# A decoder block on one core: split projection weights stored by one token block and loaded as halves by the next two, feed-forward sums held back, raw keys in another pool

## The chip, the cores and the metric

The kernel runs on one NeuronCore of a Trainium2 chip. The metric is the device time of one execution in microseconds. Every run is compared with the kernel before on the same chip.

The core's engines are called as in the profile: PE (TensorE, matmuls; PEld is its loading of weights), DVE (VectorE), ACT (ScalarE), POOL (GpSimd) and SP (SyncE, which here only issues DMAs). "PEq", "SPq" and so on are an engine's own sequencer.

## The reference, cut to what matters

One layer: two token mixers side by side (attention in a sliding window, and an mLSTM), merged by gates, then a feed-forward part. S = 2048 tokens, D = 1024. Shift, scale and gate of both halves come from a vector c.

```python
mod = c @ w_ada[l] + b_ada[l]
shift_m, scale_m, gate_m, shift_f, scale_f, gate_f = jnp.split(mod, 6, axis=-1)
h = modulate(rms_norm(x, g_pre_mix[l]), shift_m, scale_m)
proj = h @ w_in[l]
q_a, k_a, v_a, q_m, k_m, v_m, o_m, i_m, f_m, g_a, g_m = jnp.split(proj, split_points, axis=-1)
q_a = rope(q_a.reshape(B, S, N_Q_HEADS, HEAD_DIM), positions)
k_a = rope(k_a.reshape(B, S, N_KV_HEADS, HEAD_DIM), positions)
y_a = sliding_window_attention(q_a, k_a, v_a, attn_sinks[l])
...
merged = sigmoid(g_a) * (y_a @ w_branch_attn[l]) + sigmoid(g_m) * (y_m @ w_branch_mlstm[l])
mix = merged @ w_out[l]
x = x + gate_m[:, None, :] * rms_norm(mix, g_post_mix[l])
h2 = modulate(rms_norm(x, g_pre_ffn[l]), shift_f, scale_f)
ff = (silu(h2 @ w_ffn_gate[l]) * (h2 @ w_ffn_up[l])) @ w_ffn_down[l]
x = x + gate_f[:, None, :] * rms_norm(ff, g_post_ffn[l])
```

## The kernel before

**Products.** A float32 product is made of three matmuls of rounded numbers (`mm3`): each operand is a rounded half `hi` and a remainder `lo`, and hi*hi + hi*lo + lo*hi are summed. For weights the halves are made on the chip by `split`: ACT casts the raw tile to whi (L264 where the heads of q are put in pairs, L267 otherwise), and DVE subtracts it to get wlo (L265, L268). The matmuls of projections read "acc<-whi,big" and "acc<-wlo,big" in the trace.

**Blocks and stages.** The tokens are four blocks of 512 (b = 0 to 3; the words of the change call them one to four), in two superblocks of two. Each superblock runs, for each of its blocks, the projections of q (512 columns), of keys, values and the mLSTM's pre-gates (kv, 264 columns) and of the mLSTM's values (vm, 512 columns). Block 0 has its own start; in blocks 1 and 3 kv comes ahead of q, in block 2 q ahead of kv. Then come the remaining projections of both blocks in pairs, the mLSTM, the branch outputs and w_out. In the trace, the projections of block 1 lie at about 100 to 166 us, those of blocks 2 and 3 at about 693 to 870. The feed-forward part is the second half of the span.

**A token group.** `token_group` makes one such projection in four parts of two 128-row slices of the weight. A part is 24 matmuls (4 tokens' tiles x 2 slices x 3 products); four accumulators stay open for the group, and in the last part each is evacuated by ACT: q at L778 into a tx buffer, kv at L805, vm at L829 into a tx buffer and from there to memory at L830.

**What sets the order.** `run2` goes through a list of parts: the raw tile is loaded by SP (L298; kv at L784 and L785; the later pairs at L1864), then split, then its matmuls, with the loads and splits of the next parts issued ahead. There are two raw buffers (1.08 MB), and four split buffers of 512 KB, which is two pairs of halves. Beside the parts run streams, generators that `spawn` starts and a model of elapsed time steps: rotation and transposes of q and keys, the attention, the mLSTM, and `ada_stream`. A stream's work thus lands between the matmuls of the parts. Instructions of one engine run in the order of the program. SP issues all its DMAs in order and one that waits holds those behind it.

**Pools.** tx has nine buffers of 512 columns, used by q's evacuation and rotation, vm, residual rows and `ada_stream`'s weights; the raw keys and values of blocks 1 to 3 are in tx too (L804), those of block 0 in ld, a pool of four that the mLSTM's loads use later. A key tile is held until its rotation, its transpose and its stores to the attention's memory tile `at_d` (L798, L816, L818) are through. The attention of a block loads keys, values and q from there as `at` (L910), makes scores (mix<-at), masks (L943), takes the softmax on ACT (L958), transposes (L217, from tm) and multiplies with the values (mix<-tm,at).

**`ada_stream`** makes the feed-forward's scale, shift and gate from w_ada: a 256 KB load into tx each (L442), and a step later one DVE sum (L433). It is started in block 0's output and has a step each 9000 ns of the model's time; block 3 finishes it.

Of the kernel before, what the change touches and what calls it, by code (L numbers as in the profile page):

```python
# [19 lines left out]
P = 128  # L20
# [53 lines left out]
def decoder_block(ctx: ExitStack, tc: tile.TileContext, a: dict, out: bass.AP, dbg=None):  # L74
# [49 lines left out]
    def tx(shape, dtype=F32):  # L124
        return tpool.tile(shape, dtype, tag="tx", name=nm("tx"), bufs=9)
# [154 lines left out]
    def piece(raw, view, shape, mms, pair_heads=False):  # L280
        return Part(raw, lambda: split(view(raw.tile), shape, pair_heads), mms)
# [33 lines left out]
            for j in range(2):  # L315
                yield feature_tile(raw, lambda t, j=j: t[:, :, j * P:(j + 1) * P], k, i0 + j, rhs, evac)

    def token_group(srcs, nk, n, lhs, evac, pair_heads=False, stagger=1):

        acc = []  # L320
        srcs = list(srcs)
        held = []

        def make(si, k0, kc):
            def mms(wt):
                if not acc:
                    acc.extend(acc_tile() for _ in range(NT))
                held.append((wt, k0, kc))
                if len(srcs) - stagger <= si < len(srcs) - 1:
                    return  # L330
                for t in range(NT):
                    for w_, k0_, kc_ in held:
                        for j in range(kc_):
                            kk = k0_ + j
                            mm3(acc[t][:, :n], lhs(kk, t), (w_[0][:, j, :], w_[1][:, j, :]), kk == 0, kk == nk - 1)
                            yield
                    if si == len(srcs) - 1:
                        evac(t, acc[t])
                held.clear()
            return mms  # L340

        for si, (raw, view, k0, kc) in enumerate(srcs):
            yield piece(raw, view, [kc, n], make(si, k0, kc), pair_heads)

    def srcs_rows(w, nk, c0):
        for k0 in range(0, nk, 4):
# [80 lines left out]
    def ada_terms(acc, raw, k0, kn):  # L427
        for k in range(kn):
# [3 lines left out]
            else:  # L432
                V.scalar_tensor_tensor(acc, raw[:, k, :], c_, acc, op0=ALU.mult, op1=ALU.add)  # L433

    def ada_stream(parts, gap):
        for part, kind in parts:
            for ch in range(2):
                c0 = part * D + ch * 512
                acc = tm([P, 512])
                for k in range(KD):  # L440
                    raw = tx([P, 1, 512])
                    nc.sync.dma_start(raw, w_ada[:, c0:c0 + 512].rearrange("(p k) c -> p k c", k=KD)[:, k:k + 1, :])  # L442
                    yield gap
                    ada_terms(acc, raw, k, 1)
                if kind == "gate":
                    br = tx([1, 512])
                    nc.sync.dma_start(br, a["b_ada"][:, c0:c0 + 512])
                    yield gap
                    V.tensor_tensor(acc[0:1, :], acc[0:1, :], br, op=ALU.add)
                ada_tail(acc, part, ch, kind)  # L450
                yield gap
# [249 lines left out]
    def ld(shape, dtype=F32):  # L701
        t = kvp.tile([P, 512], dtype, tag="ld", name=nm("ld"), bufs=4)
        return t.rearrange("p (k c) -> p k c", k=shape[0])
# [24 lines left out]
    om_d = [tc.dram_tile([P, MH, TB], F32, name=f"om_d{i}") for i in range(NBLK)]  # L728
    g_d = [tc.dram_tile([P, 2, KD, TB], F32, name=f"g_d{i}") for i in range(NBLK)]
    y_d = [tc.dram_tile([P, 4, 4, TB], F32, name=f"y_d{i}") for i in range(NBLK)]  # L730
    LOGC = math.log(MD ** -0.5)
    LOG2 = math.log(2.0)

    def superblock(sb):
# [3 lines left out]
        def lhs_h(b):  # L738
            def lhs(kk, t):
                return tuple(p_[:, kk % 4, t * P:(t + 1) * P] for p_ in HC[f"{kk // 4 + 1}{b % 2 + 1}"])  # L740
            return lhs
# [58 lines left out]
        def evac_kv(b):  # L800
            before = [v_last]

            def evac(t, ps):
                raw = ld([1, 512])[:, 0, :] if b == 0 else tx([P, 392])  # L804
                A.copy(raw[:, :264], ps[:, :264])  # L805
                v, dv = raw[:, 128:256], raw[:, 264:392]
                n = b * NT + t
                y = rope(raw, HKV, b, t)
                for i in range(2):
                    A.copy(gt[:, t, 32 * i:32 * i + 4], raw[:, 256 + 4 * i:260 + 4 * i])  # L810
                V.tensor_tensor(dv, v, before[0], op=ALU.subtract)
                before[0] = v
                if t == NT - 1:
                    A.copy(v_last, v)
                    before[0] = v_last
                nc.sync.dma_start(at_d[n][:, AT_V + P:], dv)  # L816
                if n + 1 < S // P:
                    nc.sync.dma_start(at_d[n + 1][:, AT_V:AT_V + P], v)  # L818
                R["qk"].append(spawn(k_stream(n, y)))
            return evac  # L820

        def q_kv(b):
            raw_kv = Raw(load_kv)
            return token_group(srcs_rows(w_in, KD, C_Q), KD, 512, lhs_h(b), evac_q(b), pair_heads=True), token_group([(raw_kv, (lambda r, j=j: r[:, j:j + 2, :]), j, 2) for j in range(0, KD, 2)], KD, 264, lhs_h(b), evac_kv(b))

        def vm(b):
            def evac(t, ps):
                v = tx([P, 512])
                A.copy(v, ps)  # L829
                nc.sync.dma_start(vm_d[b][:, t, :], v)  # L830
            yield from token_group(srcs_rows(w_in, KD, C_VM), KD, 512, lhs_h(b), evac)


        def gates(b):
# [403 lines left out]
        def outputs(b):  # L1238

            def evac_a(i, ps):  # L1240
                g_ = R["g", b, 0, i // 4][:, i % 4, :]
                V.scalar_tensor_tensor(g_, g_, 1.0, ps, op0=ALU.add, op1=ALU.mult)

            m = {}

            def m_part(i, h):
                if (i, h) not in m:
                    m[i, h] = big([4, TB], F32R)
                return m[i, h]

            def evac_m(i, ps):
                g_ = R["g", b, 1, i // 4][:, i % 4, :]
                hi, lo = (m_part(j, i // 4)[:, i % 4, :] for j in range(2))
                V.scalar_tensor_tensor(g_, g_, 1.0, ps, op0=ALU.add, op1=ALU.mult)
                V.tensor_tensor(g_, g_, R["g", b, 0, i // 4][:, i % 4, :], op=ALU.add)
                A.copy(hi, g_)
                V.tensor_tensor(lo, g_, hi.bitcast(F32), op=ALU.subtract)

            def before_a():
                load_g(b, 1)  # L1260
                gate_tanh(b, 0)

            def before_m():
                end_chunks(NT * (b % 2 + 1))
                load_y(b, 2)
                if b + 1 == NBLK:
                    finish(R_ada)
                    open_hc()
                    R["hc"] = spawn(h_combine(0, *HC_FROM_MIXER), L_HC)
            yield before_a  # L1270
            first, second, *more = branch_tiles(w_ba, True, lambda: (R["y", b, 0], R["y", b, 1]), evac_a)
            yield first
            yield second
            yield more[0]
            yield before_m
            yield from more[1:]
            yield lambda: gate_tanh(b, 1)
            yield from branch_tiles(w_bm, False, lambda: (R["y", b, 2], R["y", b, 3]), evac_m)

            def before_out():  # L1280
                if b == 0:
                    finish(R["ada_m"])
                    R_ada.append(spawn(ada_stream([(4, "scale"), (3, "shift"), (5, "gate")], 9000.0)))
                if b == b1 and b + 1 < NBLK:
                    HC.clear()
                    hps[b + 1] = spawn(hprep(b + 1))
                    rope_tables(sb + 1)
                R["gg"] = big([2, D])[:, 0, :]
                nc.sync.dma_start(R["gg"], gg_m_d)
                if b == b0:  # L1290
                    end_attention(2 * NT)
                    load_y(b1, 0)
                    load_g(b1, 0)

            yield before_out

            def gg(c):
                return R["gg"][:, c]

            yield from residual_out(KD, lambda kk, t: tuple(m[i, kk // 4][:, kk % 4, t * P:(t + 1) * P] for i in range(2)),  # L1300
                                    a["w_out"][0], big, load_rows(x_d[b * TB:(b + 1) * TB, :], b + 1 == NBLK), gg, x1[b],
                                    None if b + 1 == NBLK else x1n[b])
# [25 lines left out]
            first.update(kv=kv0, evac=q_raw, rope=q_rope, rest=q_rest)  # L1328
        else:
            yield start  # L1330
            yield from q0
            yield from kv0
            yield lambda: attend(b0)
# [13 lines left out]
        def start_f():  # L1347
# [2 lines left out]
            hps["t"] = spawn(hsums(("T1", "T3")))  # L1350

        yield start_f
        pairs = [("om", 0), ("qk", 0), ("om", 1), ("qk", 1), ("ga", 0), ("qk", 2), ("ga", 1), ("qk", 3),
                 ("ga", 2), ("ga", 3), ("gm", 0), ("gm", 1), ("gm", 2), ("gm", 3)]
        for i, (kind, p) in enumerate(pairs):
# [855 lines left out]
```

## Time and profile before

| | us |
|---|---|
| median of three runs | 2673.64 (2673.51 to 2677.0) |
| the profiled execution | 2673.95 |
| its span | 2672.2 |
| PE busy | 2620.8 |
| DVE busy | 1964.5 |
| ACT busy | 1304.4 |
| POOL busy | 136.3 |

The profiled execution has 1.75 us outside its span. Its mean granted PE clock is 0.995. In the page's 40 slices PE is at 9 (90% or more) in all but the first, the last and the one from 802 to 868 us. 511.84 MB are moved, at 192 GB/s over the span. An engine's busy time counts work only; the tables of waits name, for an instruction that found its engine idle, the one that released it.

### The profile page before, as it was taken

The numbers are of one execution on the slowest core, as the hardware profiler recorded it, in microseconds if no ns is written. First come the engines' busy times: TensorE is split into PE (matmuls) and PEld (weight loads), VectorE is DVE, ScalarE is ACT, GpSimd is POOL, SyncE is SP. The second block draws the span as 40 slices with busy tenths as digits, with TensorE's granted clock in tenths as the row PEclk, the third lists the DMA queues.
The fourth block names the chain that finished last, engine by engine and source line by source line (L and its number), as shares of the span: only waits on it lengthen the run. The fifth ranks groups of instructions, "written<-read, shape, count | busy, mean of one in ns | idle before, by whom it ended". The sixth has DMA issues, their size and how long they took to land.

```text
span 2672.2 us, 36050 instructions
## 1 busy us (share of the span) xinstructions
PE 2620.8 (98%) x12546; PEld 2145.7 (80%) x12546; DVE 1964.5 (74%) x3790; ACT 1304.4 (49%) x2563; POOL 136.3 (5%) x181
## 2 busy tenths in 40 slices
PE   8999999999998999999999999999999999999998
PEld 6877788888876778888878888888778888888886
DVE  6877887768786988875777777775776767676466
ACT  6666544445764654454654443335554333333444
POOL 0000002101100000110000000000000000000000
PEclk9999999999999999999999999999999999999999
DMA  7664455987576645687675555446675323234566
GB/s 269 202 222 138 140 192 182 306 296 256 186 232 197 194 133 165 191 269 294 205 260 173 175 173 177 145 150 215 213 252 180 110 99 105 101 111 138 191 203 221
DMA packets 353062, 511.84 MB, mean 192 GB/s; under 512 B 24544, under 2 KB 213084, under 8 KB 347632
## 3 DMA queue, kind: packets, MB, share of 16 engines
q1 hardware_dynamic: 334664, 493.76, 55.6%
q10 hardware_dynamic: 18216, 15.79, 2.0%
q8 instruction: 99, 1.62, 0.2%
q14 instruction: 83, 0.68, 0.1%
HBM read 357.06 MB, written 144.02 MB: 188 GB/s over the span
## 4 chain that ended last, share of the span: by engine, by line
PE 84%; DVE 6%; DMA 5%; ACT 2%; issue 2%; POOL 0%; SPq 0%; ACTq 0%; DVEq 0%; POOLq 0%
PE acc L212 59%; PE mix L212 22%; PE mix L217 2%; DVE hl L1701 1%; DMA big<-big 1%; PE acc L90 1%; PE mix L90 1%; ACT hl L1700 1%; DMA raw<-as_d 1%; DMA big<-in_x_dram 1%; DMA at<-at_d 1%; DMA raw<-ws_d 1%; DMA at_d<-tx 1%; ACT tm L958 0%; DMA raw<-in_w_ffn_down_dram 0%
## 5 line engine op out<-in xcount | busy, mean ns | idle before, releaser
L212 PE MATMUL acc<-big,hl 128*128 128x512 f32 x3936 | 936.7, 392 | 3.6 <-ACT tx L829 1.5
L212 PEld LDWEIGHTS acc<-big,hl 128*128 128x128 f32 x3936 | 732.2, 188 | 163.5 <-issue 5.5
L1700 ACT CAST hl<-raw 128x512 fp32r<-128x512 f32 x732 | 440.6, 622 | 488.2 <-PE acc L212 219.5
L1701 DVE TENSOR_TENSOR hl<-raw,hl 128x512 fp32r<-128x512 f32 x732 | 496.4, 695 | 198.5 <-ACT hl L1700 195.9
L212 PE MATMUL acc<-whi,big 128*128 128x512 f32 (+1 forms) x1152 | 344.6, 378 | 3.7 <-ACT tx L829 1.6
L212 PE MATMUL mix<-big,hl 128*128 128x512 f32 x1056 | 263.0, 390 | 1.6 <-ACT hl L1700 0.9
L212 PEld LDWEIGHTS acc<-whi,big 128*128 128x128 f32 x1152 | 212.1, 190 | 43.3 <-ACT tx L805 2.4
L212 PE MATMUL acc<-hl,hl 128*128 128x512 f32 x1008 | 237.3, 393 | 5.9 <-DVE hl L1701 3.4
L212 PEld LDWEIGHTS mix<-big,hl 128*128 128x128 f32 x1056 | 197.8, 188 | 44.3 <-DVE hl L1701 1.8
L212 PEld LDWEIGHTS acc<-hl,hl 128*128 128x128 f32 x1008 | 186.9, 188 | 51.6 <-DVE hl L1701 8.8
L212 PE MATMUL acc<-wlo,big 128*128 128x512 f32 (+1 forms) x576 | 217.6, 379 | 3.6 <-DVE wlo L268 3.3
L212 PE MATMUL mix<-hl,hl 128*128 128x512 f32 x792 | 182.9, 391 | 1.2 <-DVE ms L456 0.4
L212 PEld LDWEIGHTS mix<-hl,hl 128*128 128x128 f32 x792 | 147.8, 188 | 35.5 <-DVE hl L1701 3.3
L212 PE MATMUL acc<-big,whi 128*128 128x512 f32 x512 | 157.3, 393 | 0.0
L268 DVE TENSOR_TENSOR wlo<-raw,whi 128x1024 fp32r<-128x1024 f32 (+1 forms) x92 | 106.9, 1163 | 67.2 <-ACT whi L267 61.6
L267 ACT CAST whi<-raw 128x1024 fp32r<-128x1024 f32 (+1 forms) x92 | 91.9, 1000 | 117.3 <-PE acc L212 111.2
L212 PEld LDWEIGHTS acc<-wlo,big 128*128 128x128 f32 x576 | 109.9, 191 | 24.1 <-DVE wlo L268 4.8
L458 POOL TENSOR_TENSOR rs<-ms,halves 128x1 f32<-128x1 f32 (+1 forms) x56 | 41.6, 754 | 1640.2 <-DVE ms L456 1592.3
L212 PE MATMUL mix<-hcT4h,hl 128*128 128x512 f32 x352 | 115.6, 389 | 0.7 <-ACT hl L1700 0.7
L212 PE MATMUL acc<-hcT2h,hl 128*128 128x512 f32 x352 | 115.5, 389 | 0.0
L212 PEld LDWEIGHTS acc<-big,whi 128*128 128x128 f32 x512 | 95.3, 188 | 19.3
L212 PE MATMUL acc<-big,wlo 128*128 128x512 f32 x256 | 97.5, 392 | 0.0
(377 smaller groups left out, 3542.0 us busy)
## 6 DMA issues: line engine op xcount, KB each, us to landing
raw<-in_w_in_dram SPq DMA_DIRECT2D x46, 1024.0 KB, 5.2
as_d<-w SPq DMA_DIRECT2D x154, 256.0 KB, 2.0
raw<-as_d SPq DMA_DIRECT2D x70, 512.0 KB, 3.7
raw<-in_w_ffn_gate_dram SPq DMA_DIRECT2D x22, 1024.0 KB, 5.7
raw<-in_w_ffn_up_dram SPq DMA_DIRECT2D x22, 1024.0 KB, 5.9
raw<-ws_d SPq DMA_DIRECT2D x40, 512.0 KB, 4.5
tx<-in_w_ada_dram SPq DMA_DIRECT2D x64, 256.0 KB, 5.2
g_d<-tx SPq DMA_DIRECT2D x64, 256.0 KB, 2.5
```

Source lines behind the costliest of these rows:

```text
L90: self.last = tc.keep_in_program_order(f(*p, **k)).ins
L212: T.matmul(o, lhsT=lhsT, rhs=rhs, start=start, stop=stop, skip_group_check=resumed)
L217: T.transpose(o, i, ident[:k, :k])
L267: A.copy(hv, src)
L268: V.tensor_tensor(lv, src, hv.bitcast(F32), op=ALU.subtract)
L458: G.tensor_tensor(r[:, :n], ms[:, :n], nhalf[:, :n], op=ALU.pow)
L1700: A.copy(v(hi), src)
L1701: V.tensor_tensor(v(lo), src, v(hi).bitcast(F32), op=ALU.subtract)
```

## The change

Four edits go together.

1. In block 1, `token_group` stores both halves of each part, right after they are split, to memory tiles `W_D["q"]`, `W_D["kv"]`, `W_D["vm"]` (24 stores by SP, of 512 KB, kv of 264 KB).
2. Blocks 2 and 3 take q, kv and vm from there through `kept_weights`. Even parts of q and vm (and two parts of kv at once) come as one load into a raw buffer, odd parts of q and vm as two loads into a pair of split buffers. Nothing is cast or subtracted for them; the pairing of q's heads is in what was stored. The matmuls of the former then read "acc<-raw,big".
3. `ada_stream` goes by 6500 ns a step in place of 9000, and `hold(True)` at the start of the second superblock pauses it until `start_f`, behind its block projections.
4. The raw keys of all blocks are in ld.

```diff
@@ token_group @@
+    def kept_weights(name):
+        n = 528 if name == "kv" else 1024
+        for j0 in range(0, 4, 2):
+            for j in ((j0,) if name == "kv" else (j0, j0 + 1)):
+                def load(j=j):
+                    src = W_D[name]
+                    if name != "kv" and j % 2:
+                        parts = [split_tile(x) for x in ("whi", "wlo")]
+                        for i in range(2):
+                            nc.sync.dma_start(parts[i].bitcast(F32), src[:, j, i, :])
+                        return [parts]
+                    m = 2 if name == "kv" else 1
+                    t = wpool.tile([P, RAWC], F32R, tag="raw", name=nm("raw"))
+                    v = t[:, :m * 2 * n].rearrange("p (m i c) -> p m i c", m=m, i=2)
+                    nc.sync.dma_start(v.bitcast(F32), src[:, j:j + m, :, :])
+                    return [[v[:, q, i, :] for i in range(2)] for q in range(m)]
+                raw = Raw(load)
+                for q in range(2 if name == "kv" else 1):
+                    yield raw, q, 2 * (j + q), 2
...
-            yield piece(raw, view, [kc, n], make(si, k0, kc), pair_heads)
+            if kept:
+                def ready(raw=raw, q=view):
+                    return tuple(v.rearrange("p (k c) -> p k c", k=2) for v in raw.tile[q])
+                yield Part(raw, ready, make(si, k0, kc))
+                continue
+            part = piece(raw, view, [kc, n], make(si, k0, kc), pair_heads)
+            if store:
+                def prep(do=part.prep, si=si, kc=kc):
+                    made = do()
+                    for i, v in enumerate(made):
+                        nc.sync.dma_start(W_D[store][:, si, i, :].rearrange("p (k c) -> p k c", k=kc), v.bitcast(F32))
+                    return made
+                part.prep = prep
+            yield part
@@ ada_stream @@
+                    while held[0]:
+                        yield 1000.0
@@ evac_kv @@
-                raw = ld([1, 512])[:, 0, :] if b == 0 else tx([P, 392])
+                raw = ld([1, 512])[:, 0, :]
@@ q_kv (vm likewise) @@
+            if b > 1:
+                q = token_group(kept_weights("q"), KD, 512, lhs_h(b), evac_q(b), kept=True)
+            else:
+                q = token_group(srcs_rows(w_in, KD, C_Q), KD, 512, lhs_h(b), evac_q(b), pair_heads=True, store="q" if b else None)
@@ before_out @@
-                    R_ada.append(spawn(ada_stream([(4, "scale"), (3, "shift"), (5, "gate")], 9000.0)))
+                    R_ada.append(spawn(ada_stream([(4, "scale"), (3, "shift"), (5, "gate")], 6500.0)))
@@ second superblock's start @@
             yield start
+            yield lambda: hold(True)
             yield from q0
@@ pairs @@
         yield start_f
+        yield lambda: hold(False)
```

PE in block 3, the attention of block 2's last tokens beside block 3's projection of q, before. "at" holds loaded keys, values and q; "tm" softmax weights; "tx" rotated keys and q that wait for their transposes; "acc<-whi" is the projection.

```order
L212 MATMUL acc_8458<-whi_8452,big_7106 128x512
L212 MATMUL mix_7855<-at_7779 128x256 x6
L212 MATMUL mix_7926<-at_7826 128x256
L217 MATMUL mix_7988<-ident,tm_7834 128x128 x4
L212 MATMUL mix_8036<-tm_7993,at_7779 64x256 x2
L217 MATMUL mix_8063<-ident,tm_7924 128x128 x4
L212 MATMUL mix_8106<-tm_8068,at_7826 64x256 x2
L217 MATMUL mix_8293<-ident,tx_8223 128x128
L212 MATMUL acc_8459<-whi_8386,big_7105 128x512
```

The rows shown are the first of each kind; between the two projection rows stand 30 score matmuls, 16 transposes of softmax weights, three of rotated keys and 16 products with values, and no projection. PE at the same place now:

```order
L212 MATMUL mix_7834<-at_7761 128x256 x6
L212 MATMUL acc_8217<-raw_8133,big_7151 128x512
L212 MATMUL mix_7901<-at_7805 128x256
L212 MATMUL acc_8219<-raw_8133,big_7151 128x512 x2
L217 MATMUL mix_7960<-ident,tm_7813 128x128 x4
L212 MATMUL acc_8383<-raw_8271,big_7128 128x512 x2
L212 MATMUL mix_8006<-tm_7965,at_7761 64x256 x2
L217 MATMUL mix_8051<-ident,tm_7900 128x128 x4
L212 MATMUL acc_8383<-raw_8325,big_7151 128x512 x2
L212 MATMUL mix_8069<-tm_8038,at_7805 64x256 x2
L217 MATMUL mix_8223<-ident,ld_8144 128x128
L212 MATMUL acc_8383<-wlo_8380,big_7151 128x512
```

Each piece of attention now has 8 to 33 projection matmuls behind it, of q (acc 8217, 8219) and already of vm (acc 8383), and the keys' transposes read ld.

ACT at the start of block 1's q, before; "acc" here are the accumulators of kv, L958 is the softmax of block 0's attention.

```order
L264 CAST whi_1425<-raw_1059 128x2x4x64 x2
L805 COPY tx_1439<-acc_1133 128x264
L941 COPY tm_1354<-mix_1374 128x256
L958 ACTIVATE tm_1268,sums_1266<-tm_1268,nmx_1265 128x128
L958 ACTIVATE tm_1269,sums_1266<-tm_1269,nmx_1265 128x128 x4
L805 COPY tx_1457<-acc_1134 128x264
L264 CAST whi_1522<-raw_1059 128x2x4x64 x2
```

And now, where L805, L941, L958 and L895 are L847, L992, L1009 and L946:

```order
L992 COPY tm_1365<-mix_1385 128x256
L1009 ACTIVATE tm_1279,sums_1277<-tm_1279,nmx_1276 128x128
L1009 ACTIVATE tm_1280,sums_1277<-tm_1280,nmx_1276 128x128 x4
L847 COPY ld_1452<-acc_1140 128x264
L946 ACTIVATE ex_1350<-ex_1350 128x48
L264 CAST whi_1436<-raw_1062 128x2x4x64 x2
L847 COPY ld_1470<-acc_1141 128x264
```

The first casts of q's weights (x2: one for each of a part's two slices) moved from ahead of the softmax and of the first evacuation to behind both.

SP in block 1 now, at the end of kv; L374 is a store of halves, L298 the load of the second half of q's weights, L860 and L858 the stores of values (L818 and L816 before).

```order
L1091 DMA vmt_176<-vm_d_210 128x4x128
L374 DMA w_kv_d<-whi_1193 128x528
L374 DMA w_kv_d<-wlo_1259 128x528
L298 DMA raw_1264<-in_w_in_dram 128x4x512
L860 DMA at_d_195<-ld_1452 128x128
L374 DMA w_q_d<-whi_1436 128x1024
L374 DMA w_q_d<-wlo_1437 128x1024
```

That load now stands behind all eight stores of kv, and the stores of q and vm stand between the loads that follow.

More of the change, by code (lines that the diff above doesn't have):

```diff
@@ L316, in feature_tiles, with token_group @@
                 yield feature_tile(raw, lambda t, j=j: t[:, :, j * P:(j + 1) * P], k, i0 + j, rhs, evac)
-    def token_group(srcs, nk, n, lhs, evac, pair_heads=False, stagger=1):
+    def kept_weights(name):
[17 more added lines that the diff above has]
+                    yield raw, q, 2 * (j + q), 2
+    def token_group(srcs, nk, n, lhs, evac, pair_heads=False, stagger=1, store=None, kept=False):
         acc = []
@@ L433, in ada_terms, with hold @@
                 V.scalar_tensor_tensor(acc, raw[:, k, :], c_, acc, op0=ALU.mult, op1=ALU.add)
+    held = [False]
+    def hold(on):
+        held[0] = on
     def ada_stream(parts, gap):
@@ L730, in decoder_block @@
     y_d = [tc.dram_tile([P, 4, 4, TB], F32, name=f"y_d{i}") for i in range(NBLK)]
+    W_D = {x: tc.dram_tile([P, 4, 2, 528 if x == "kv" else 1024], F32, name=f"w_{x}_d") for x in ("q", "kv", "vm")}
     LOGC = math.log(MD ** -0.5)
@@ L822, in q_kv @@
         def q_kv(b):
+            if b > 1:
+                q = token_group(kept_weights("q"), KD, 512, lhs_h(b), evac_q(b), kept=True)
+            else:
+                q = token_group(srcs_rows(w_in, KD, C_Q), KD, 512, lhs_h(b), evac_q(b), pair_heads=True, store="q" if b else None)
+            if b > 1:
+                return q, token_group(kept_weights("kv"), KD, 264, lhs_h(b), evac_kv(b), kept=True)
             raw_kv = Raw(load_kv)
-            return token_group(srcs_rows(w_in, KD, C_Q), KD, 512, lhs_h(b), evac_q(b), pair_heads=True), token_group([(raw_kv, (lambda r, j=j: r[:, j:j + 2, :]), j, 2) for j in range(0, KD, 2)], KD, 264, lhs_h(b), evac_kv(b))
+            return q, token_group([(raw_kv, (lambda r, j=j: r[:, j:j + 2, :]), j, 2) for j in range(0, KD, 2)], KD, 264, lhs_h(b), evac_kv(b), store="kv" if b else None)
         def vm(b):
@@ L830, in evac @@
                 nc.sync.dma_start(vm_d[b][:, t, :], v)
-            yield from token_group(srcs_rows(w_in, KD, C_VM), KD, 512, lhs_h(b), evac)
+            if b > 1:
+                yield from token_group(kept_weights("vm"), KD, 512, lhs_h(b), evac, kept=True)
+            else:
+                yield from token_group(srcs_rows(w_in, KD, C_VM), KD, 512, lhs_h(b), evac, store="vm" if b else None)
         def gates(b):
```

## The prediction

> **What bounds the kernel now.** I read the page's busy times first, then the busy times and clock in stretches of the span, then TensorE's waits in the stretches where it isn't full, last the timeline around the longest of them.
>
> ```profile
> PE 2620.8 (98%) x12546; PEld 2145.7 (80%) x12546; DVE 1964.5 (74%) x3790; ACT 1304.4 (49%) x2563; POOL 136.3 (5%) x181
> ```
>
> TensorE is busy for 2620.8 of 2672.2 us. No change that leaves its matmuls alone, as this one does, can win more than the other 51.4 us and what a lowered clock costs. Where they lie (columns: stretch, its length, then busy time and instructions of PE, PEld, DVE, ACT and POOL, granted clock, DMA share, GB/s):
>
> ```profile
> 95.00:170.00 75.00, 70.82 (x418) 58.24 (x418) 57.01 (x156) 47.01 (x144) 7.65 (x8) 0.95 0.62 194
> 105.00:122.00 17.00, 14.58 (x104) 13.17 (x103) 15.24 (x45) 7.04 (x18) 0.00 (x0) 0.80 0.65 218
> 690.00:820.00 130.00, 123.81 (x703) 102.14 (x702) 101.30 (x253) 81.59 (x193) 12.55 (x15) 0.99 0.66 216
> 740.00:800.00 60.00, 55.19 (x316) 46.93 (x316) 50.24 (x147) 37.65 (x107) 4.69 (x4) 0.97 0.74 240
> 765.00:780.00 15.00, 12.97 (x93) 11.93 (x92) 14.81 (x32) 7.29 (x17) 0.00 (x0) 0.89 0.80 285
> 800.00:870.00 70.00, 61.27 (x334) 44.33 (x333) 47.66 (x109) 34.62 (x87) 4.69 (x5) 0.93 0.62 196
> 818.00:842.00 24.00, 16.49 (x93) 10.23 (x93) 13.01 (x37) 14.81 (x53) 4.69 (x5) 0.79 0.40 123
> 960.00:1350.00 390.00, 390.00 (x1909) 327.52 (x1909) 301.46 (x610) 196.90 (x342) 34.65 (x32) 1.00 0.66 216
> ```
>
> The row at 960 is what most of the kernel looks like: full at clock 1.00. The projections of blocks 2 and 3 are not: 740 to 800 lacks 4.8 us and 800 to 870 lacks 8.7. The lowered clock adds 12.97 x 0.11 = 1.4 us at 765 and 16.49 x 0.21 = 3.5 at 818, together 4.9. What ends TensorE's waits from 660 to 960 (engine, line, what was waited for; us in total, times, longest):
>
> ```profile
> PE mix L212 <- DMA at<-at_d: 4.4, 2, 3.1
> PE mix L217 <- POOL tm L961: 3.3, 3, 2.8
> PE acc L212 <- DVE wlo L268: 3.3, 3, 2.3
> PE acc L212 <- ACT tx L829: 2.8, 2, 1.6
> PE mix L212 <- DVE tm L974: 0.9, 1, 0.9
> PE acc L212 <- ACT hl L1700: 0.6, 1, 0.6
> PE mix L217 <- DVE tx L758: 0.5, 1, 0.5
> PE acc L212 <- ACT whi L264: 0.5, 1, 0.5
> PE mix L217 <- DVE tm L943: 0.2, 1, 0.2
> ```
>
> That is 16.5 us. Only 3.3 + 0.5 = 3.8 of them are the splits of weights. The largest group is one place in block 3:
>
> ```profile
> 809.05 0.59 ACT L778 COPY tx<-acc 128x512 f32<-128x512 f32 x1
> 839.98 0.59 ACT L778 COPY tx<-acc 128x512 f32<-128x512 f32 x1
> ...
> 819.85 0.97 PE L212 MATMUL mix<-at 64*128 64x256 f32 x6
> 823.94 2.93 PE L212 MATMUL mix<-at 64*128 64x256 f32 x24 [3.13 <-DMA at<-at_d]
> 834.31 1.12 PE L217 MATMUL mix<-ident,tm 128*128 128x128 f32 x4 [2.77 <-POOL tm L961]
> 841.25 0.47 PE L212 MATMUL acc<-whi,big 128*128 128x512 f32 x1
> ```
>
> The evacuation of q stops for 31 us between two L778 copies, because their tx buffers are taken. With the accumulators full, TensorE has no projection matmul from 819.9 to 841.25 and runs attention alone, waiting for its loads and its chain: 3.1 + 3.3 + 0.9 + 0.2 = **7.5 us** of the nine rows.
>
> **The change: blocks 2 and 3.** Splits there, each row with count and minimum/median/maximum in ns:
>
> ```profile
> L264 ACT CAST whi<-raw x16: 602/617/628, 693.0 to 799.8; 128x512 fp32r<-128x512 f32 x16
> L265 DVE TENSOR_TENSOR wlo<-raw,whi x16: 626/684/1529, 693.6 to 801.9; 128x512 fp32r<-128x512 f32 x16
> L267 ACT CAST whi<-raw x16: 634/838/1063, 717.2 to 851.5; 128x528 fp32r<-128x528 f32 x8, 128x1024 fp32r<-128x1024 f32 x8
> L268 DVE TENSOR_TENSOR wlo<-raw,whi x16: 686/962/1226, 719.7 to 854.5; 128x528 fp32r<-128x528 f32 x8, 128x1024 fp32r<-128x1024 f32 x8
> L433 DVE SCALAR_TENSOR_TENSOR tm<-tx,c_sb,tm x8: 725/733/748, 723.9 to 795.6; 128x512 f32<-128x512 f32 x8
> ```
>
> Removed from ScalarE: 16 x 0.617 + 16 x 0.838 = 23 us; from VectorE: 16 x 0.684 + 16 x 0.962 = 26, and the paused sums 8 x 0.733 = 6. Almost all of it lay beside TensorE; what counts are the waits. The 3.8 us of the splits go. In the lump two things change: raw keys go to ld and the paused stream holds no tx, so both takers of tx other than q and its rotation leave. By the changed order projections then stand between the attention pieces. Of the 7.5 us I take 5.5 as gained, keeping 2 for a first attention load that is late anyway. The L829 wait (2.8) is an evacuation behind other ScalarE work, which loses 23 us: half, 1.4. With waits this short the clock should mostly hold: 4 of its 4.9. **Sum: 3.8 + 5.5 + 1.4 + 4 = 14.7 gained.** Bounds: from 3.8 (lump, evacuation and clock stay) to 3.8 + 7.5 + 2.8 + 4.9 = 19.
>
> The paused sums and their 256 KB loads go to stretches like 960 to 1350, where VectorE has 390 - 301.46 = 89 us free and TensorE loses nothing: 0, at worst the 6 us again.
>
> The loads double: q and vm need 128 x 1024 x 4 bytes x 2 halves x 4 parts = 4.2 MB each and kv 2.16, so 10.55 MB a block in place of half of that.
>
> ```profile
> raw<-in_w_in_dram SPq DMA_DIRECT2D x46, 1024.0 KB, 5.2
> vm_d<-tx SPq DMA_DIRECT2D x16, 256.0 KB, 7.1
> at<-at_d ACTq DMA_DIRECT2D x8, 896.0 KB, 7.0
> 122.55 0.39 PE L212 MATMUL acc<-wlo,big 128*128 128x512 f32 x1
> 123.25 0.39 PE L212 MATMUL acc<-wlo,big 128*128 128x512 f32 x1
> ```
>
> Three matmuls start in 0.70 us, so a part (24) takes 5.6; its 1 MB lands in 5.2 and may be fetched up to four parts ahead. From 690 to 820 the DMA engines are idle for 0.34 x 130 = 44 us; the extra 10.55 MB, at the 216/0.66 = 327 GB/s of their busy time, take 32. I cost it at 0. The cover is thin at 740 to 800 (share 0.74), and the loads it would slow are the attention's, whose waits are 4.4 now: bound +5, as if they doubled.
>
> **The change: block 1.** Here work is only added.
>
> ```profile
> 117.86 1.14 ACT L264 CAST whi<-raw 128x512 fp32r<-128x512 f32 x2 [3.57 <-PE acc L212]
> 125.03 0.36 ACT L805 COPY tx<-acc 128x264 f32<-128x264 f32 x1
> ...
> 110.34 0.69 PE L217 MATMUL mix<-ident,tm 68*128 68x68 f32 x4 [2.42 <-DVE tm L868]
> 125.44 0.50 PE L212 MATMUL acc<-whi,big 128*128 128x512 f32 x1 [1.56 <-ACT tx L805]
> ```
>
> A split pair is now free only when its stores have landed. By the order of ScalarE the first cast of q, at 117.86 before, comes behind the softmax and the key copy at 125.03. So the first wlo matmul of q starts near 125.03 + 0.36 + 0.62 (one cast) + 0.68 (one difference) = 126.7, not 122.55. Before, q stood for 1.56 behind that copy anyway: 126.7 - 122.55 - 1.56 = **+2.6**. TensorE then waits over 3 us in one piece. The wait of 2.42 at 110.34 is followed by the stretch at 0.80, which costs 14.58 x 0.20 = **2.9**; I take the same. For stores beside loads **+0.5**. Sum: **+6.0**. Its bounds are -1.6 (the wait of 1.56 vanishes, nothing comes) and, from the DMA engines, 10.7: they are idle for 0.38 x 75 = 28.5 us from 95 to 170; 10.55 MB at 194/0.62 = 313 GB/s take 33.7, so 5.2 don't fit (2.6 + 2.9 + 5.2).
>
> The Trainium skill speaks against this part: "DMA: Bandwidth & Descriptors", section "Issuing engines are not separate DMA queues", says that DMAs of all issuers run on the same 16 engines and interleave. So the K/V loads that ScalarE issues get no shelter from SyncE's stores; by that rule the 5.2, not 0.5, would be added and the time 4.7 later. No row here has such stores beside such loads.
>
> **The sum.** The profiled execution took 2673.95 (span 2672.2), 0.31 above the median 2673.64. 2673.95 - 14.7 + 6.0 = **2665.2**.
>
> **Rivals.** *Only the splits' waits go* (the lump comes back from another shortage, the clock stays): 2673.95 - 3.8 + 6.0 = 2676.1. For it: at 834.31 the waits are POOL's, not a missing buffer's. Against: 31 us between two L778 copies.
> *Short waits leave the clock alone*, so all 4.9 come back and block 1 pays no 2.9: 2665.2 - 0.9 - 2.9 = 2661.4. Against it: 2.42 us stood ahead of the row at 0.80.
> By the Trainium skill, "TensorE: Matmul & The Clock Gate", section "HAM oscillation", only gaps above about 3.4 us throttle; the 2.42 us above disagree with it.
> *K/V loads collide with the doubled weight loads*: +5, 2670.2. For it: share 0.80 at 765. Against: 44 idle us for 32.
> *Slots wait for stores* (the slower side): block 1 has two pairs, so a part's stores must land within the time of two parts, 11.2 us. The 256 KB store above takes 7.1 beside other traffic, and 1 MB of halves may take twice that, 14.2: 3 us late on each of the 8 parts of q and vm, +24, 2689.2. It begins once stores land later than 11.2 us; it decides from 8.75/8 = 1.1 us past that, where the time passes that of before.
> *The halves come late*: the change doesn't do what it says, the wait for wlo becomes one for a load. At 1 us on each of the 16 parts of q and vm: 2681.2. Against: fetched four parts ahead.
>
> **How the numbers follow.** Forecast 0.50, its own range 2659 to 2668.5; splits alone 0.16; clock spared 0.10; collision 0.09; slots 0.10; late halves 0.05. A measurement of this kernel tells about 0.2%, 5.3 us, from no change. Forecast and spared clock are faster by more: 0.60. Splits alone and collision lie within: 0.25. Slots and late halves: 0.15 slower. The range reaches from the full gain, 2673.95 - 19, to 2677, past the case of splits alone; outside it lie the 0.15 and a little.
>
> **What would show it.** Right: no L264 or L267 from 690 to 870; the two L778 copies a few us apart and projection matmuls between 820 and 841; the clock of 800 to 870 near 1.00; in block 1 a wait of some 3 us ahead of the first q matmul, and a stretch below 0.9 after it. Wrong: waits for DMA raw, whi or wlo (halves late), L264 or L265 in block 1 idle until a store has landed (slots), at<-at_d above 4.4 us (collision), or a new hole beyond 870, which I see no cause for.

## The result and the profile after

The changed kernel took 2667.18 us in the median of 17 runs (2664.28 to 2675.15), the kernel before 2673.94 in 17 runs (2670.89 to 2677.32). The ratio is 0.9976 with a 95% interval of 0.9969 to 0.9983: some 6.5 us faster by the ratio (6.8 by the medians), where 8.75 were forecast. The profiled execution of the change took 2670.21 (span 2668.1), 3 us above its median, so times are compared by medians and places by the traces.

Busy time by stretches, the columns as before (stretch, length, PE, PEld, DVE, ACT, POOL, clock, DMA share, GB/s):

```profile
95.00:170.00 75.00, 69.31 (x404) 55.91 (x404) 49.89 (x139) 40.63 (x119) 4.23 (x4) 0.91 0.88 304
660.00:740.00 80.00, 80.00 (x437) 69.00 (x437) 55.40 (x119) 54.53 (x106) 9.04 (x13) 1.00 0.72 251
740.00:800.00 60.00, 60.00 (x373) 49.11 (x372) 40.00 (x134) 33.64 (x98) 4.17 (x4) 1.00 0.90 308
800.00:870.00 70.00, 61.50 (x319) 46.92 (x318) 41.27 (x93) 30.39 (x84) 4.69 (x5) 0.95 0.68 233
818.00:842.00 24.00, 23.15 (x126) 17.40 (x125) 7.56 (x17) 6.72 (x19) 2.61 (x3) 1.00 0.41 129
```

Read the rows in pairs with those of before. 740 to 800 lost 4.8 us of TensorE and now loses none, at full clock, although the DMA share rose from 0.74 to 0.90. The hole at 818 to 842 is shut: 0.85 us idle in place of 7.5. Yet 800 to 870 as a whole still lacks 8.5, against 8.7 before. TensorE's waits from 660 to 960:

```profile
PE acc L212 <- ACT tx L877: 3.7, 1, 3.7
PE acc L212 <- DVE hl L1754: 3.4, 2, 3.0
PE acc L212 <- ACT tx L820: 0.8, 1, 0.8
PE mix L212 <- DMA at<-at_d: 0.6, 1, 0.6
```

Of the nine rows before, none for a split of q, kv or vm is left, nor the attention's chain. The first row is new; the second, "hl", is the split of the pairs' weights, which both kernels make, and has grown from 0.6. They lie where block 3's projections end and the pairs begin; the timeline there (start, length, engine, line, tiles; in brackets the wait before it):

```profile
840.31 0.59 ACT L820 COPY tx<-acc 128x512 f32<-128x512 f32 x1
840.95 1.65 PE L212 MATMUL acc<-raw,big 128*128 128x512 f32 x6 [0.85 <-ACT tx L820]
842.63 0.39 SPq L1917 DMA_DIRECT2D raw<-in_w_in_dram  x1
849.99 1.14 ACT L1753 CAST hl<-raw 128x512 fp32r<-128x512 f32 x2 [2.22 <-DMA raw<-in_w_in_dram]
851.04 1.06 ACT L877 COPY tx<-acc 128x512 f32<-128x512 f32 x2
851.66 1.90 PE L212 MATMUL acc<-big,hl 128*128 128x512 f32 x4 [3.65 <-ACT tx L877]
864.47 4.84 PE L212 MATMUL acc<-big,hl 128*128 128x512 f32 x13 [2.96 <-DVE hl L1754]
```

Read it as a chain. q's fourth evacuation gets its tx buffer at 840.31; only then can vm's first part run its last six matmuls, from a raw buffer that holds halves. That buffer is free at their end, and the pairs' first load is issued at 842.63; in the kernel before it was at 815.24, since a split had freed the buffer. The load's cast comes at 849.99, vm's evacuations stand behind it, and TensorE waits. The wait at 864.47 is for the pairs' next split; VectorE, which makes it, is busy for 10.02 of the 10.10 us from 855.40 to 865.50 (row in the last section).

In block 1, waits ahead of q's matmuls:

```profile
110.92 0.45 PE L217 MATMUL mix<-ident,tm 68*128 68x68 f32 x4 [2.70 <-DVE tm L919]
125.15 1.12 PE L217 MATMUL mix<-ident,tm 128*128 128x128 f32 x4 [2.23 <-POOL tm L1012]
127.52 0.80 PE L212 MATMUL acc<-wlo,big 128*128 128x512 f32 x1 [0.77 <-DVE wlo L265]
```

The wait of "some 3 us" is there, 2.23 + 0.77, first for the softmax, as nothing of q was ready to fill in. The first wlo matmul of q is at 127.52; 126.7 was worked out.

### The profile page after: what moved, and what is told of

The parts are those of the page before. It is cut to its first block, busy times and chain, and to the rows that moved or that the text cites. A ratio compares the mean times of both kernels' runs of the same rounds, so it can differ in the third digit from the quotient of the medians.

```text
span 2668.1 us, 36043 instructions
## 1 busy us (share of the span) xinstructions
PE 2619.0 (98%) x12546; PEld 2143.4 (80%) x12546; DVE 1940.2 (73%) x3758; ACT 1282.5 (48%) x2531; POOL 134.4 (5%) x181
## 4 chain that ended last, share of the span: by engine, by line
PE 88%; DVE 4%; DMA 4%; ACT 2%; issue 1%; POOL 0%; SPq 0%; ACTq 0%; DVEq 0%; POOLq 0%
PE acc L212 63%; PE mix L212 22%; PE mix L217 2%; DVE hl L1754 1%; PE acc L90 1%; PE mix L90 1%; DMA raw<-in_w_ffn_down_dram 1%; ACT hl L1753 1%; DMA raw<-as_d 1%; DMA raw<-ws_d 0%; DMA g_d<-tx 0%; DVE big L583 0%; ACT tm L1009 0%; DMA big<-in_x_dram 0%; DMA at<-at_d 0%
## 5 line engine op out<-in xcount | busy, mean ns | idle before, releaser
L212 PE MATMUL acc<-whi,big 128*128 128x512 f32 (+1 forms) x896 | 280.9, 389 | 0.0
L212 PEld LDWEIGHTS acc<-whi,big 128*128 128x128 f32 x896 | 167.9, 191 | 34.4 <-issue 1.9
L212 PE MATMUL acc<-wlo,big 128*128 128x512 f32 (+1 forms) x448 | 174.4, 390 | 1.4 <-DVE wlo L265 0.8
L268 DVE TENSOR_TENSOR wlo<-raw,whi 128x1024 fp32r<-128x1024 f32 (+1 forms) x76 | 91.5, 1204 | 63.1 <-ACT whi L267 56.5
L267 ACT CAST whi<-raw 128x1024 fp32r<-128x1024 f32 (+1 forms) x76 | 78.6, 1034 | 105.4 <-PE acc L212 89.1
L212 PEld LDWEIGHTS acc<-wlo,big 128*128 128x128 f32 x448 | 85.4, 191 | 19.6 <-DVE wlo L268 1.4
```

The costliest lines, as they stand in the source:

```text
L212: T.matmul(o, lhsT=lhsT, rhs=rhs, start=start, stop=stop, skip_group_check=resumed)
L267: A.copy(hv, src)
L268: V.tensor_tensor(lv, src, hv.bitcast(F32), op=ALU.subtract)
```

## The experiments

All times are medians, each with five rounds beside the kernel before (whose own medians in these groups were 2673.5 to 2674.7). "Halves" are edits 1 and 2, "pause" is edit 3, "ld" edit 4.

| run | what it has | median us | ratio to before, 95% interval |
|---|---|---|---|
| the change | halves, pause, ld | 2667.18 | 0.9976 (0.9969 to 0.9983) |
| e1 | pause, ld | 2671.58 | 0.9990 (0.9981 to 0.9998) |
| e2 | pause, ld, stores without loads | 2670.60 | 0.9984 (0.9975 to 0.9993) |
| e3 | halves | 2667.21 | 0.9967 (0.9955 to 0.9980) |
| e4 | the change without vm's halves | 2667.66 | 0.9980 (0.9972 to 0.9989) |
| e5 | halves, ld | 2673.74 | 0.9995 (0.9986 to 1.0004) |
| e6 | halves, pause | 2658.05 | 0.9940 (0.9928 to 0.9953) |
| e7 | the change without kv's halves | 2664.87 | 0.9966 (0.9954 to 0.9977) |
| e8 | the change, block 3 splits vm | 2673.20 | 0.9990 (0.9981 to 1.0000) |
| e9 | pause | 2666.81 | 0.9972 (0.9961 to 0.9982) |
| e10 | pause, stores without loads | 2669.45 | 0.9979 (0.9970 to 0.9988) |
| e11 | halves of q and vm, pause | 2653.93 | 0.9924 (0.9911 to 0.9936) |
| e12 | ld | 2671.17 | 0.9992 (0.9982 to 1.0001) |

**First group: which edits carry the gain.** Edits against the changed kernel:

```diff
 e1: no stores, no kept weights (q shown; kv and vm alike)
-            if b > 1:
+            if b > 9:
-... store="q" if b else None)
+... store=None)
 e2: the same, but with the stores of block 1 (q shown; kv and vm alike)
+... store="q" if b == 1 else None)
 e3: raw keys as before, no pause, 9000 a step
-                raw = ld([1, 512])[:, 0, :]
+                raw = ld([1, 512])[:, 0, :] if b == 0 else tx([P, 392])
-            yield lambda: hold(True)
+            yield lambda: hold(False)
 e4: vm is not stored, and is split in every block
```

> The pause of the feed-forward sums and the raw keys in ld, without stored weights: every block splits its own. Theory A (tx buffers made the hole of block 3, and the two small edits empty them): the stretch 818 to 842 has under 2 us idle, the waits for whi and wlo stay (about 4 us), block 1 is as before: 2666 to 2668, as fast as the whole change. Rival B (the stored halves carry the gain): the hole stays, 2672 to 2674.

Measured 2671.58, 0.4 under rival B's range and far from theory A's: rival B. Without halves TensorE still has 13 us (828.8 to 841.5) without a projection matmul, filled a little better than before. The waits for whi and wlo did not stay, as theory A had it: from 660 to 960 there is none.

> As the run without stored weights, but block 1 still stores its halves, which nobody loads. Theory A (block 1 pays for the stores and for their place in its order): 4 to 6 us above that run, some 2672, granted clock from 95 to 170 near 0.91. Rival B (what block 1 loses lies beside other work): the same time as that run within 2 us.

Measured 2670.60, 1 us under e1 with overlapping intervals: rival B by the time. In the trace the waits of block 1 are there (2.2 and 1.1), and the clock from 95 to 170 is 0.93, against 0.95 in e1.

> Stored halves alone: raw keys in tx as before, the sums are not paused and go by 9000. Theory A: the waits for whi and wlo go (3.8 us), the hole of block 3 stays in part, block 1 pays its 4 us: 2672 to 2675. Rival B (the stored halves carry the gain): 2667.

Measured 2667.21: rival B. Halves alone give what the whole change gives, and the hole is gone with the keys still in tx:

```profile
818.00:842.00 24.00, 24.00 (x129) 17.58 (x127) 13.79 (x35) 10.68 (x37) 3.88 (x5) 1.00 0.54 169
```

> The change without vm: q and kv are stored and loaded as halves, vm is loaded and split in every block. Theory A (a raw buffer that holds halves is freed by the matmuls, no longer by the split, so the first weights of the pairs come late behind vm of block 3): the 3.7 and 3.0 us waits at 847 to 865 go, with the lowered clock behind them, some waits for vm's wlo come back, and 4.2 MB of stores leave block 1: 2660 to 2664. Rival B (those waits are evacuations short of tx, whatever the raw buffers do): they stay, 2666 to 2668.

A hit on the place and a miss on the time. The waits of 3.7 and 3.0 are gone, but ten rows of waits, none longer than 1.2 us, stand from 660 to 960 instead, 8.2 us together; 2667.66. With vm split again, a stretch of 10.2 us without a projection matmul is back as well (830.0 to 840.2).

**Second group: the two small edits.**

```diff
 e5: against the change
-            yield lambda: hold(True)
+            yield lambda: hold(False)
-... "gate")], 6500.0)))
+... "gate")], 9000.0)))
 e6: against the change
-                raw = ld([1, 512])[:, 0, :]
+                raw = ld([1, 512])[:, 0, :] if b == 0 else tx([P, 392])
 e7: kv is not stored, and is split in every block
-            if b > 1:
+            if b > 9:
                 return q, token_group(kept_weights("kv"), ...)
-... store="kv" if b else None)
+... store=None)
 e8: vm
-            if b > 1:
+            if b == 2:
-... store="vm" if b else None)
+... store="vm" if b == 1 else None)
```

> Stored halves and raw keys in ld, the feed-forward sums run through as before (9000 a step). Theory C (the halves carry the gain; the pause buys nothing because its VectorE work and its two or three tx buffers are not what TensorE waits for): 2666 to 2668, the same as the whole change and as halves alone. Rival A (the pause matters): over 2670, with waits for tx in 740 to 870.

Measured 2673.74: rival A on the time. The pause is worth 6.6 us here. Without it, halves and ld together win nothing that can be measured. The place is 740 to 800, where 5.6 us are idle at clock 0.94. TensorE's waits in that stretch are for the attention's chain (softmax, masks and evacuated tiles of tm), not for tx as rival A had it; the one long wait for tx, 4.4 us, is at the start of the pairs.

> Stored halves and the pause, raw keys in tx as before. Theory C (the keys' pool is not what opens the hole of block 3): 2666 to 2668, no hole over 2 us from 815 to 845. Rival A (the keys' pool removes the hole): the hole back, TensorE without projection matmuls for over 10 us, 2671 or more.

Measured 2658.05, 8 us under what any theory had, and 9.1 under the change. No hole came back. Its stretches, then all its waits from 660 to 960:

```profile
95.00:170.00 75.00, 69.20 (x413) 57.13 (x412) 55.38 (x151) 43.48 (x128) 6.41 (x6) 0.93 0.90 317
740.00:800.00 60.00, 59.45 (x370) 48.62 (x369) 41.29 (x139) 35.62 (x105) 4.16 (x4) 1.00 0.89 307
800.00:870.00 70.00, 69.79 (x385) 54.16 (x385) 48.52 (x106) 34.44 (x93) 4.68 (x5) 1.00 0.74 252
...
PE mix L212 <- DMA at<-at_d: 0.5, 1, 0.5
PE acc L212 <- ACT tx L877: 0.4, 1, 0.4
PE mix L217 <- POOL tm L1012: 0.4, 1, 0.4
PE acc L212 <- DVE big L583: 0.2, 1, 0.2
```

16.5 us of waits before are 1.5 here, and the clock is whole: what the prediction hoped for in blocks 2 and 3, without the edit that it credited. Most of ld's 9 us lie in 800 to 870: there the change has 8.5 us idle and 3.1 of clock lost (61.50 x 0.05), this run 0.2 idle at full clock. The timeline shows how:

```profile
812.21 0.59 ACT L820 COPY tx<-acc 128x512 f32<-128x512 f32 x1 [1.71 <-PE acc L212]
828.13 0.59 ACT L820 COPY tx<-acc 128x512 f32<-128x512 f32 x1
829.41 0.64 ACT L820 COPY tx<-acc 128x512 f32<-128x512 f32 x1
831.33 0.59 ACT L820 COPY tx<-acc 128x512 f32<-128x512 f32 x1 [1.28 <-DVE tx L837]
...
838.66 0.39 SPq L1917 DMA_DIRECT2D raw<-in_w_in_dram  x1
```

With keys in tx, one token of q is evacuated early, the other three by 831.9, and the pairs' load goes out at 838.66. With keys in ld three tokens of q are evacuated by 815, the fourth waits until 840.31, and the load goes out at 842.63, too late by the 3.65 us above.

> The change without kv's halves: kv is loaded and split in every block, so no stores stand in the stretch from 95 to 118. Theory D (block 1 pays through the first stores, those of kv, which hold back q's first split and its second load): the 2.2 and 0.8 us waits ahead of q go back to about 1.6, one lowered-clock period of 3.4 or 6.8 us goes with them, waits for kv's wlo of 1 us come back: 2663 to 2666. Rival E (the place of q's first cast behind the softmax is enough by itself): waits as in the whole change, 2667.

Measured 2664.87: theory D, in its range. Block 1 waits 1.6 us in place of 2.2 + 0.8, and its clock from 95 to 170 is 0.98 in place of 0.91. The time is 2.3 us under the change's, with overlapping intervals, so the place says more here than the time.

> The change, but block 3 alone loads vm raw and splits it; the stores stay. Theory F (a raw buffer with halves is freed by matmuls and so the pairs' first weights come late): the pairs' first load is issued near 820 instead of 842.6, the 3.7 and 3.0 us waits at 847 to 865 go, 2661 to 2665. Rival G (what goes there comes back as other waits, as in the run without vm's halves): 2666 to 2668.

Theory F on the place: the pairs' load is issued at 824.92 and the waits at 847 to 865 are gone. Miss on the time: 2673.20. The attention of block 3 now waits for its softmax later,

```profile
877.61 1.09 PE L217 MATMUL mix<-ident,tm 128*128 128x128 f32 x8 [1.71 <-POOL tm L1012]
923.61 2.82 PE L217 MATMUL mix<-ident,tm 128*128 128x128 f32 x12 [3.00 <-POOL tm L1012]
```

where the change has no wait at all. From 740 to 800, ahead of the part that was edited, its clock is 0.94 where the change has 1.00. Both together outweigh what 800 to 870 won. e1 waits at the same two places in its trace; e2, which differs from e1 by the stores alone, does not, so that splitting vm brings these waits is not shown.

**Third group: with the keys in tx.** e9, e10 and e11 are e1, e2 and e7 with the raw keys' line of before; e12 is the kernel before with only that line changed.

> The pause (and 6500 a step) alone: no stores, every block splits, raw keys in tx. Theory H (without halves q of block 3 still ends ahead of the attention and stands without tx): a stretch of over 8 us without projection matmuls between 815 and 845 stays, waits for whi and wlo stay: 2668 to 2672. Rival P (the pause by itself is what made the run with keys in tx fast): 2662 or less.

Measured 2666.81, between the two: below H's range, above P's. H was right on the hole: no projection matmul from 816.3 to 831.9.

> The pause, and block 1 stores its halves, which nobody loads; keys in tx. Theory A (the stores cost block 1 waits and clock): 2 to 4 us over the run with the pause alone, with 2.2 and 1.1 us waits at 124 to 127. Rival B (they cost nothing to the end of the program): within 1.5 us of it.

Measured 2669.45, 2.6 over e9, with 2.2 and 1.1 us waits at 124 to 127: what theory A asked for. The intervals overlap, so the price of the stores is not settled beyond "small".

> The pause, keys in tx, halves of q and vm only; kv is split in every block. Theory D (the first stores cost block 1 some 2 us): 2655 to 2657, below the run with keys in tx and all halves (2658). Rival (kv's splits in blocks 2 and 3 come back as waits for wlo and cost as much): 2658 to 2662.

Measured 2653.93, 1 us better than theory D's range and the fastest version, 4.1 under e6 (the intervals overlap only at their ends). The stretch from 95 to 170, and TensorE's waits from 100 to 130:

```profile
95.00:170.00 75.00, 72.12 (x446) 59.25 (x445) 59.06 (x157) 47.45 (x143) 6.79 (x7) 1.00 0.87 307
...
PE acc L212 <- ACT tx L847: 1.6, 1, 1.6
PE mix L217 <- DVE tm L919: 1.1, 1, 1.1
PE acc L212 <- DVE wlo L265: 0.2, 1, 0.2
```

No clock is lost in block 1, where the kernel before has 0.95 and the change 0.91. The 1.1 for L919 (L868 before) is 2.0 to 2.7 in the other traces, e7's among them, which has the same edit with ld; why it is shorter here is not shown, so not all of the 4.1 need be kv's stores.

> The kernel before with the raw keys in ld and nothing else. Theory L (keys in ld let three tokens of q take the tx buffers that the keys' rotation and stores need, in every version alike): slower by 5 to 9 us, 2679 to 2683, the last q transposes of block 3 later than in the kernel before. Rival M (it costs only beside the halves or the pause, where the paused stream's tx were free): within 2 us of the kernel before. Rival A (it removes the hole of block 3, as the prediction had it): 2668 to 2671.

Measured 2671.17, 2.4 us under the kernel before of its group, with an interval that just reaches 1. Theory L is wrong. The time lies between the ranges of rivals M and A and cannot tell them apart; the place can, since the hole is there, 24 us without a projection matmul. That leaves rival M:

```profile
818.00:842.00 24.00, 15.90 (x104) 10.71 (x102) 11.64 (x33) 14.09 (x50) 4.17 (x4) 0.86 0.31 88
```

## Why the prediction came out as it did

By its medians the change won 6.8 of the forecast 8.75 us and moved as said. Two terms in it were wrong with opposite signs: the pause gained and the raw keys in ld lost, by like amounts. That the total came near the forecast is in part luck.

**The splits' waits** (3.8 gained): right for the change, where none is left from 660 to 960. But they are not the halves' alone to win: e1, without halves, has none either, e2 0.9 and e9 1.9. So the halves are enough for this term, but not needed for it.

**The lump** (5.5 gained): right in size at its place, 7.5 us to 0.85, wrong in cause. The step that failed is "raw keys go to ld and the paused stream holds no tx, so both takers of tx other than q and its rotation leave". Those two edits without halves keep the hole, together (13 us without projections in e1) and one by one (16 in e9, 24 in e12); it was 21 before. Every version in which block 3 loads halves of q and vm (the change, e3, e5, e6, e7, e11) has no such stretch over 3 us from 815 to 845, whichever pool the keys are in; e4 and e8, in which block 3 splits vm, have 10.2 and 7.2 there. In e3 and e6 three of q's evacuations still come 16 us after the first, behind the key tiles that hold tx. So the missing buffers remained; what changed is that the order with halves puts attention pieces between the parts of q and vm, instead of leaving them for the time in which q stands. The prediction has this order in its next sentence, but gave the credit to the buffers.

**The pause** (0, at worst 6 us lost): wrong. By the medians it is worth 6.6 us beside halves and ld (e5 to the change), 9.2 beside halves (e3 to e6) and 7.9 alone (e9); by the ratios to the kernel before 5, 7 and 7.5. In e3, without it, 740 to 800 has 6.8 idle us at clock 0.94; e6 has 0.55 at 1.00:

```profile
740.00:800.00 60.00, 53.21 (x317) 44.50 (x316) 43.96 (x144) 34.09 (x99) 4.42 (x4) 0.94 0.94 325
```

The prediction counted its VectorE time and gave its tx buffers no price of their own. Whether the buffers or the order that it moves is what counts was not separated, nor the pause from the shorter step that goes with it.

**Raw keys in ld** (part of the lump's gain): a loss of 9.1 us beside halves and pause (the change against e6), 6.5 beside halves (e5 against e3), 4.8 beside the pause (e1 against e9, intervals just touching), nothing alone (e12). "A new hole beyond 870, which I see no cause for" was looked for in the wrong place: it opened at 847 to 865. Its last link, a raw buffer that the matmuls free and no longer the split, was in the change's own text; alone it costs little, as e6 has it too and waits 0.4 us there. What ld changes is alike in all traces: the eight versions with ld evacuate three tokens of q early and the fourth 20 to 41 us later, the six with keys in tx one token early and the others from 16 to 31 us later. In e5, e7 and e8 the fourth ends a wait for a store to `at_d`, which frees a tx buffer. That q takes tx buffers which the keys' chain then lacks is the likely reading, not a tested one. Why the order of a version with ld sets the keys' transposes later is not shown by these runs.

**L829 and the clock** (1.4 and 4 gained): the evacuation's wait went from 2.8 to nothing at its old place and came back as 3.7 in the new hole. Of 4.9 us of clock, 61.50 x 0.05 = 3.1 are still lost from 800 to 870.

**Block 1** (+6.0): the mechanism was right and the size a little high, mostly in the first term: 2.6 of waits was 1.5, 2.9 of clock was 2.7, and no price of the stores beside the loads can be told apart. Waits from 100 to 130 went from 4.2 (2.4 + 1.6 + 0.2) to 5.7 and the clock's loss from 95 to 170 from 70.82 x 0.05 = 3.5 to 69.31 x 0.09 = 6.2, together 4.2. In times the stores cost 2.6 us (e10 over e9) or nothing (e2 against e1). The rival with slots that wait for stores showed once, on ScalarE: a cast of L267 waited 2.1 us for a store of kv's halves (landing takes 7.0 us in the median). None of TensorE's waits from 95 to 180 over 0.8 us is for a split, so it did not cost what that rival asked.

By the Trainium skill, "DMA: Bandwidth & Descriptors", section "Issuing engines are not separate DMA queues", DMAs of all issuers run on the same engines and interleave; this case agrees as far as it goes, as the DMA share from 95 to 170 rose from 0.62 to 0.88 with the stores. The 5.2 us that the prediction let that rule add were not paid in e2 or e10.

**The doubled loads** (0): right. The attention's loads made TensorE wait 0.6 in place of 4.4, at a DMA share of 0.90. Halves came late only in e3, where TensorE waited 3.0 us for kv's at a DMA share of 0.94, and in e7, 0.9 us for those of q and vm.

## What to carry to other kernels

Where several edits go together, price each on its own and in pairs: here one of three took back more than half of what the other two won, and alone it showed nothing. When a buffer that a short step used to free is read by the matmuls instead, follow who loads into it next. When a pool is short, giving one user another pool moves the shortage to whoever is next in the order, which can be worse; look at the order, not only at the count.

## What was not expected of the hardware

Waits of 2 to 3 us were enough to lower the clock. After the waits of 3.65 and 2.96 in the change, and from the end of the wait of 2.23 in block 1 on, with one of 0.77 inside, the granted clock was one half:

```profile
851.90:855.30 3.40, 2.93 (x7) 1.77 (x7) 3.37 (x8) 3.40 (x8) 0.00 (x0) 0.50 1.03 429
855.40:865.50 10.10, 7.14 (x37) 5.12 (x36) 10.02 (x19) 5.63 (x12) 0.00 (x0) 1.00 1.04 402
865.60:869.00 3.40, 3.40 (x10) 2.50 (x8) 3.34 (x9) 0.62 (x1) 0.00 (x0) 0.50 0.68 210
124.90:131.70 6.80, 5.78 (x18) 4.43 (x18) 5.77 (x24) 6.80 (x34) 2.62 (x4) 0.50 0.58 212
```

The lowered stretches last 3.4 us or twice that, so by these rows a wait of 3 us costs an estimated 1.7 or 3.4 us more (half of 3.4 or 6.8). By the Trainium skill, "TensorE: Matmul & The Clock Gate", section "HAM oscillation", gaps above about 3.4 us do this; the length of a lowered stretch agrees with that figure, the 2.96 us wait does not.
